# The context's products with group B's input columns in a pass of their own, the S5 units beside the latent tokens' pass

## The chip, the cores and the metric

The kernel runs on one core of one Trainium2 chip. The time is the device time of one execution in microseconds (us), the median of three runs. Every engine (TensorE, VectorE, ScalarE, GpSimd, SyncE) works through its own queue of instructions in order, and waits at an instruction whose inputs aren't there yet.

## The reference

One layer of a network over 1024 latent tokens with 2048 features and 256 context tokens. Cut to what matters:

```
proj_x = modulate(x,   shift_x, scale_x) @ w_in          # 1024 x 2048 @ 2048 x 5120
ub_c   = modulate(ctx, shift_c, scale_c) @ w_in[:, B]    # 256 x 2048 @ 2048 x 1024
u, v, za, ub_x, zb = split(proj_x)                       # 1024 columns each
ya = u' * (w_s @ LN(v') + b) * silu(za)                  # group A: position mixing in 8 heads
yb = S5(ub_x, ub_c)                                      # group B: 64 groups, scan in both directions,
                                                         #   latent scans start from the context's state
yb = glu(yb) * silu(zb)
gate = silu(c) @ w_ada[:, 4096:] + b_ada[4096:]          # one row of 2048
out = LN(alpha * x + gate * (concat(ya, yb) @ w_out)) * ln_g + ln_b
```

So the weights' columns of group B (ub) are multiplied with the latent tokens and with the context; the S5 scan needs both products.

## The kernel before, in words

**Products.** All large products are float32 split in two parts: ScalarE copies a raw chunk of weights to a rounded part (`whi`), VectorE subtracts it from the raw chunk to get the rest (`wlo`). The inputs have such parts too (`xT` for the latent tokens, `cT` for the context, each a pair). A k-step is three passes: hi x hi, hi x lo, lo x hi. A chunk of weights is 128 x 1024 (512 KB) and holds 8 k-steps of one block of 128 output columns; a block is two chunks. `block` (L827) does one block for the two halves of the latent tokens: two PSUM banks of 128 x 512 (tag `mm`), so six matmuls of 512 columns for a k-step. With `extra` it adds a third bank (tag `sb`), and three matmuls of 256 columns for a k-step.

**Weights.** `Weights` (L547 on) loads raw chunks on SP's queue and splits them. `wget` (L654) hands out a chunk, issues the load two chunks ahead and the split of the next chunk. There are two buffers each for `whi`, `wlo` and the raw chunk, so the split of the next chunk waits until the matmuls of the one before the present are done.

**Order of the blocks** in the input projection: four of v, the first of zb, eight of ub (group B), four of v, then u and za of each head in turn, then the rest of zb. Behind them come the GLU and the output projection.

**Side tasks.** Everything beside the weights' matmuls is written as generators. `pump` (L672) moves each task on by one step after each k-step. A model of the engines' clocks (`ck.pe`, `ck.dve`, ...) that each issued instruction advances decides when a task goes on: `until(t)` waits for the model's TensorE to reach t, `room` for VectorE to be at most 2500 ns ahead. `drain` (L691) pumps the tasks without issuing a block in between, and advances the model's TensorE clock by 1300 ns each time. All of this happens when the kernel is built; on the chip the order on each engine is fixed.

The tasks that matter here:
- `bias_task` (L1044): for each of 8 heads a load of w_sp (`ws`, two buffers) and b_sp (`bs`, one buffer), a matmul with ones, one VectorE operation, and a store on ScalarE's queue.
- `gate_task` (L1058): the gate's row. Loads of 512 KB of w_gate, one VectorE multiply-add per 128 rows of it into `acc`, at the end of a stretch of columns a matmul that adds up the partitions.
- `ub_evac` (L1092): after each ub block ScalarE copies the three banks to `us` and stores it in scratch with eight DMAs on its own queue (tile `tmp_ub`).
- `s5_task` (L1111): first the S5 tables (some 300 small VectorE operations, results to scratch), then 32 units of two groups each. A unit on VectorE: `make_w`, `make_e`, `make_t`, `rot`, `scan`, `back`. On TensorE: `pe_b` (input products, 24 matmuls `sb<-uu,uw`), `pe_z` (taps, 30 small matmuls into `sy`), `pe_y` (outputs, `sy<-uu,uk` and `sy<-us,ut`). A unit reads its input `uu` from `tmp_ub`. This task starts behind the last ub block, beside the second half of v.

In the ub pass the code reads

```
    tasks.append(bias_task())
    for m in range(8):
        o, e = block(("ub", m), extra=cxT)
        ub_evac(m, o, e)
        if m == 0:
            tasks.append(gate_task())
    drain()
```

Of the kernel before, what the change touches and what calls it, by code (L numbers as in the profile page):

```python
# [13 lines left out]
OP = mybir.AluOpType  # L14
# [573 lines left out]
def build(tc, a, out, scratch):  # L588
# [32 lines left out]
    col0 = {"u": 0, "v": 8, "za": 16, "ub": 24, "zb": 32}  # L621
# [30 lines left out]
    W.alloc_raw = lambda i: wpool.tile([128, 1024], FT, name="wraw", tag="whi" if i == 2 else "wraw")  # L652
# [174 lines left out]
    def block(key, order=(0, 1), extra=None):  # L827
        o = [bank("mm", 4) for _ in range(2)]
        e = bank("sb", 2) if extra else None
        n = 0  # L830
        for c in order:
            hi, lo = wget((key, c))
            for kk in range(8):
                k = 8 * c + kk
                wt = (hi[:, kk * 128:kk * 128 + 128], lo[:, kk * 128:kk * 128 + 128])
                bs = list(zip(o, xT))
                if extra:
                    bs.append((e[:, :256], extra))
                kstep(bs, wt, k, n == 0, n == 15)
                n += 1  # L840
                pump()
        return o, e
# [191 lines left out]
    o, _ = block(("v", 3))  # L1034
    vb.append(o)
    o, _ = block(("zb", 0))
# [6 lines left out]

# [14 lines left out]
    def gate_task():  # L1058

        for c in range(2):  # L1060
            cols = slice(1024 * c, 1024 * c + 1024)
            acc = st_p.tile([128, 1024], FT, name="acc", tag="sta")
            w = {}

            def load(i):
                w[i] = (st_p.tile([128, 1024], FT, name="gw", tag="stb") if i % 2 else
                        us_p.tile([128, 1024], FT, name="gw", bufs=1))
                SP.dma_start(w[i], a["w_gate"][i * 128:i * 128 + 128, cols])
            load(0)
            for i in range(16):  # L1070
                if i < 15:
                    load(i + 1)
                yield from wait(2)
                if i:
                    V.scalar_tensor_tensor(acc, w[i], sc[:, 0, i:i + 1], acc, op0=OP.mult, op1=OP.add)
                else:
                    V.tensor_scalar(acc, w[0], sc[:, 0, 0:1], None, op0=OP.mult)
                yield
            br = us_p.tile([128, 1024], FT, name="gw", bufs=1)
            SP.dma_start(br[0:1], a["b_gate"][None, cols])  # L1080
            yield from wait(3)
            yield from until(ck.dve + 2000)
            for h in halves:
                ps = bank("ps", 1)
                T.matmul(ps, ones, acc[:, h], start=True, stop=True)
                yield from wait(2)
                V.tensor_add(br[0:1, h], ps[0:1], br[0:1, h])
            SP.dma_start(scratch["gate"][None, cols], br[0:1])
# [3 lines left out]
    def ub_evac(m, o, e):  # L1092
        us = us_p.tile([128, 8, NK], FT, name="us", bufs=1)
        S.activation(us[:, :, 0:KC].rearrange("p j k -> p k j"), e[:, :256].rearrange("p (k j) -> p k j", j=8), AF.Copy)
        for h in range(2):
            S.activation(us[:, :, KC + 64 * h:KC + 64 * h + 64].rearrange("p j k -> p k j"),
                         o[h].rearrange("p (k j) -> p k j", j=8), AF.Copy)
# [10 lines left out]
    cx_es.close()  # L1108


    def s5_task():  # L1111
# [22 lines left out]
        for u in range(3):  # L1134
            s5.load_u(u)
# [39 lines left out]
        def outputs(u):  # L1175
            yield from after(u, tk)
            yield from until(max(tb[u], tk[u]) + 700)
            yield from bank_held()
            s5.pe_y(u)
            yield from until(ck.pe + 500)  # L1180
            s5.evac_y(u)
            if u + 3 < NU:
                s5.load_u(u + 3)
            held.clear()
            out_.add(u)

# [44 lines left out]
    tasks.append(s5t)  # L1231

# [3 lines left out]
    def head_in(h):  # L1236
        vh = s2.tile([128, 8, 128], FT, name="vh")
# [12 lines left out]
    def head_out(h, ug, zs):  # L1250
        vh, ws, bp = hv.pop(h)
        yield from wait(2)
        for c in range(2):
# [4 lines left out]
            tm = s2.tile([128, 4, 128], FT, name="tm")  # L1258
# [16 lines left out]
    for m in range(4, 8):  # L1275
        o, _ = block(("v", m))
        start(v_last(o) if m == 7 else v_out(m, o))
    for h in range(8):
        o, _ = block(("u", h))
# [3 lines left out]
        o, _ = block(("za", h))  # L1283
# [25 lines left out]
    for m in range(1, 8):  # L1309
        if m == 7:  # L1310
            drain(s5t)
            s5_es.close()
            sb_open()
            s2_es.close()
            tasks.append(y5_task(g1_es.enter_context(tc.tile_pool(name="g1", bufs=1))))
        o, _ = block(("zb", m))
        if m == 1:
            drain(ho)
        zb_out(m, o)
# [252 lines left out]
```

## Time and profile before

| | us |
|---|---|
| median of 3 runs | 1667.15 (1666.43 to 1670.48) |
| profiled execution | 1667.93 |
| its span, first to last instruction | 1666.2 |
| TensorE busy | 1602.8 (96%) |
| VectorE busy | 1048.7 (63%) |
| ScalarE busy | 510.1 (31%) |
| GpSimd busy | 157.3 (9%) |

The profile's names: PE is TensorE's matmuls, PEld its weight loads, DVE VectorE, ACT ScalarE, POOL GpSimd; ACTq and SPq are DMA issues on ScalarE's and SyncE's queues. All engine instructions go through one helper and so have the line L521; they are told apart by their tiles, written output<-input. A matmul's duration holds its way through the array, and matmuls overlap: their pace is read from their starts. PEclk is the clock granted to TensorE as a share of 2.4 GHz. In order of time the blocks of group B (with `cT`) lie between 213 and 443 us, the tables between about 454 and 566 us, the S5 units between 566 and 1175 us.

### The profile page before, as it was taken

What the parts mean: (1) busy time and instruction counts of PE and PEld (TensorE: products, weight loads), DVE (VectorE), ACT (ScalarE), POOL (GpSimd) and SP (SyncE); (2) the same over time, 40 slices, a digit from 0 to 9 for tenths busy, and PEclk for the clock granted to TensorE, in tenths of its full rate; (3) what the DMA queues carried; (4) which work ended last, traced back from release to release, by engine and by line L of the source; (5) the groups of instructions that cost most, each with busy time, mean ns of one, the idle gap of its engine ahead of it and who ended that gap; (6) DMA issues with size and microseconds to landing.
All of it is one profiled execution on the core that took longest, in us unless ns stands there. A gap on an engine that the chain in (4) does not pass through costs nothing.

```text
span 1666.2 us, 23176 instructions
## 1 busy us (share of the span) xinstructions
PE 1602.8 (96%) x9056; PEld 1298.0 (78%) x9056; DVE 1048.7 (63%) x1914; ACT 510.1 (31%) x833; POOL 157.3 (9%) x214
## 2 busy tenths in 40 slices
PE   4999999999999899999999999999999999999995
PEld 1556888888878788788888888777888888887895
DVE  8542613332299598988988888896376544456447
ACT  2544631111121322332233323223443412133222
POOL 0000000000000021212212211122000000012004
PEclk9999999999999999999999999999999999999998
DMA  9885325444223533443444344333445533365332
GB/s 336 311 315 201 115 90 173 146 150 157 85 77 131 161 112 102 130 121 98 136 110 117 110 134 119 107 106 104 159 141 171 200 101 127 133 221 180 100 119 101
DMA packets 119494, 241.80 MB, mean 145 GB/s; under 512 B 33364, under 2 KB 63188, under 8 KB 117592
## 3 DMA queue, kind: packets, MB, share of 16 engines
q1 hardware_dynamic: 94808, 215.88, 39.4%
q10 hardware_dynamic: 14336, 14.68, 2.7%
q0 software_dynamic: 10240, 9.76, 2.5%
q8 instruction: 71, 1.16, 0.3%
q14 instruction: 39, 0.32, 0.1%
HBM read 203.97 MB, written 36.12 MB: 144 GB/s over the span
## 4 chain that ended last, share of the span: by engine, by line
PE 79%; DVE 7%; DMA 7%; issue 3%; ACT 2%; SPq 1%; ACTq 1%; POOL 0%; POOLq 0%; DVEq 0%
PE mm L521 56%; PE sb L521 10%; PE sy L521 8%; PE ps L521 4%; DMA uk<-tmp_z 3%; DMA tmp_z<-zs 1%; DMA wraw<-in_w_out_dram 1%; DVE wlo L521 1%; DVE lnw L521 1%; DVE stats L521 1%; DVE z L521 1%; ACT whi L521 1%; DVE t L521 1%; DVE xn L521 1%; DMA xn<-in_x_dram 1%
## 5 line engine op out<-in xcount | busy, mean ns | idle before, releaser
L521 PE MATMUL mm<-xT,whi 128*128 128x512 f32 x2496 | 717.3, 401 | 2.1 <-ACT whi L521 1.2
L521 PEld LDWEIGHTS mm<-xT,whi 128*128 128x128 f32 x2496 | 442.4, 189 | 99.2 <-issue 7.0
L521 DVE TENSOR_TENSOR wlo<-wraw,whi 128x1024 fp32r<-128x1024 f32 (+1 forms) x156 | 191.6, 1230 | 393.6 <-ACT whi L521 390.6
L521 PE MATMUL mm<-xT,wlo 128*128 128x512 f32 x1248 | 393.9, 393 | 3.3 <-DVE wlo L521 3.2
L521 ACT ACTIVATE whi<-wraw 128x1024 fp32r<-128x1024 f32 (+1 forms) x156 | 161.4, 1036 | 428.6 <-PE mm L521 197.2
L521 PEld LDWEIGHTS mm<-xT,wlo 128*128 128x128 f32 x1248 | 227.0, 189 | 52.2 <-DVE wlo L521 4.6
L405 POOL DMA_DIRECT2D tmp_z<-zs x64 | 42.5, 669 | 708.5 <-DVE uw L521 579.2
L521 PE MATMUL mm<-whi,ya 128*128 128x512 f32 (+1 forms) x320 | 83.5, 347 | 0.0
L521 PE MATMUL mm<-whi,yb 128*128 128x512 f32 (+1 forms) x320 | 83.5, 347 | 0.0
L521 POOL TENSOR_TENSOR z<-z,lnb 128x1024 f32<-128x1024 f32 (+1 forms) x16 | 36.8, 2307 | 452.1 <-ACT z L521 452.1
L521 PE MATMUL sb<-cT,whi 128*128 128x256 f32 x256 | 72.9, 285 | 0.0
L521 PE MATMUL mm<-y,whi 128*128 128x512 f32 x256 | 68.4, 389 | 0.0
L521 PEld LDWEIGHTS mm<-whi,yb 128*128 128x128 f32 x320 | 56.4, 189 | 7.5
L521 PEld LDWEIGHTS mm<-whi,ya 128*128 128x128 f32 x320 | 56.4, 189 | 7.4
L477 POOL DMA_DIRECT2D tmp_y<-ys x64 | 38.6, 608 | 233.7 <-ACT ys L521 232.9
L521 PE MATMUL sy<-ada,cs 128*32 128x512 f32 x256 | 41.4, 630 | 19.4 <-DMA ada<-in_w_mod_dram 19.4
L521 ACT ACT_TABLE_LOAD x39 | 50.0, 1283 | 32.6 <-issue 29.8
L521 PEld LDWEIGHTS sb<-uu,uw 128*64 128x64 f32 x768 | 46.7, 140 | 15.5 <-issue 10.5
L521 DVE SCALAR_TENSOR_TENSOR acc<-gw,sc,acc 128x1024 f32<-128x1024 f32 x30 | 38.5, 1283 | 30.8 <-DMA gw<-in_w_gate_dram 30.6
L521 PEld LDWEIGHTS sb<-cT,whi 128*128 128x128 f32 x256 | 47.9, 187 | 10.7
L521 PE MATMUL mm<-wlo,yb 128*128 128x512 f32 (+1 forms) x160 | 55.7, 348 | 0.3 <-DVE wlo L521 0.3
L521 PEld LDWEIGHTS mm<-y,whi 128*128 128x128 f32 x256 | 48.0, 188 | 10.0
(262 smaller groups left out, 2287.2 us busy)
## 6 DMA issues: line engine op xcount, KB each, us to landing
wraw<-in_w_in_dram SPq DMA_DIRECT2D x77, 512.0 KB
ada<-in_w_mod_dram SPq DMA_DIRECT2D x64, 512.0 KB
wraw<-in_w_out_dram SPq DMA_DIRECT2D x56, 512.0 KB
gw<-in_w_gate_dram SPq DMA_DIRECT2D x32, 512.0 KB
xn<-in_x_dram SPq DMA_DIRECT2D x16, 512.0 KB
upf<-tmp_pf SPq DMA_DIRECT2D x32, 256.0 KB
ubb<-in_b_c_dram SPq DMA_DIRECT2D x32, 256.0 KB
tmp_ub<-us ACTq DMA_DIRECT2D x64, 80.0 KB
```

The costliest lines, as they stand in the source:

```text
L405: nc.gpsimd.dma_start(dap(d["z5"], (z["g0"] + q) * 32 * 144, [[72, 2], [144, 32], [1, 72]]), zs[64 * q:64 * q + 64])
L477: nc.gpsimd.dma_start(dap(d["y5"], (g0 + g) * 16384, [[128, 8], [1024, 16], [1, 128]]), ys[:, g])
L521: r = f(*args, **kw)
```

## The change

The order of the blocks gets eight more, `cx`, between zb 0 and ub. They have the same weights as ub. A `cx` block does the context's products alone (three matmuls of 256 columns for a k-step), so group B's weights are loaded and split twice. Each `cx` block is copied to `usc` and stored with eight DMAs of its own, each ub block likewise with eight. A third raw buffer (`craw`) serves every third chunk of the `cx` pass. `bias_task` runs beside the `cx` blocks, `s5_task` and `gate_task` start before the first ub block; a unit's load of `uu` is issued only when the ub block that it reads has been stored (`ub_there`). The gate's row is made in four stretches of 512 columns instead of two of 1024, with half the length of each VectorE operation and twice as many. Behind the last ub block `drain(gt_)` issues steps of all tasks until the gate's task has ended.

```
-    blocks = ([("v", m) for m in range(4)] + [("zb", 0)] + [("ub", m) for m in range(8)]
+    blocks = ([("v", m) for m in range(4)] + [("zb", 0)] + [("cx", m) for m in range(8)] + [("ub", m) for m in range(8)]
...
+    def wraw(i):
+        if i % 3 == 2 and first[("cx", 0), 0] + 3 < i <= first[("cx", 7), 1]:
+            return us_p.tile([128, 1024], FT, name="craw", bufs=1)
+        return wpool.tile([128, 1024], FT, name="wraw", tag="whi" if i == 2 else "wraw")
+    W.alloc_raw = wraw
...
-        for c in range(2):
-            cols = slice(1024 * c, 1024 * c + 1024)
-            acc = st_p.tile([128, 1024], FT, name="acc", tag="sta")
+        for c in range(4):
+            acc = s2.tile([128, 512], FT, name="acc", tag="tm")
...
+                for j in range(2):
+                    k = 2 * i + j
+                    if k:
+                        V.scalar_tensor_tensor(acc, w[i][:, j], sc[:, 0, k:k + 1], acc, op0=OP.mult, op1=OP.add)
...
             yield from until(ck.dve + 2000)
...
+            T.matmul(ps, ones, acc, start=True, stop=True)
...
+    def ub_out(m, us, k0, n):
         for j in range(8):
-            S.dma_start(dap(scratch["ub"], (8 * m * 128 + 16 * (7 - j)) * NK, [[128 * NK, 8], [NK, 16], [1, NK]]), us[:, j])
+            S.dma_start(dap(scratch["ub"], (8 * m * 128 + 16 * (7 - j)) * NK + k0, [[128 * NK, 8], [NK, 16], [1, n]]),
+                        us[:, j])
     tasks.append(bias_task())
     for m in range(8):
-        o, e = block(("ub", m), extra=cxT)
-        ub_evac(m, o, e)
-        if m == 0:
-            tasks.append(gate_task())
+        e = bank("sb", 2)
+        for c in range(2):
+            hi, lo = wget((("cx", m), c))
+            for kk in range(8):
+                wt = (hi[:, kk * 128:kk * 128 + 128], lo[:, kk * 128:kk * 128 + 128])
+                kstep([(e[:, :256], cxT)], wt, 8 * c + kk, c + kk == 0, c == 1 and kk == 7)
+                pump()
+        us = us_p.tile([128, 8, KC], FT, name="usc")
+        S.activation(us.rearrange("p j k -> p k j"), e[:, :256].rearrange("p (k j) -> p k j", j=8), AF.Copy)
+        ub_out(m, us, 0, KC)
     drain()
...
         for u in range(3):
+            yield from ub_there(u)
             s5.load_u(u)
...
     s5t = s5_task()
     tasks.append(s5t)
+    gt_ = gate_task()
+    tasks.append(gt_)
+    for m in range(8):
+        o = block(("ub", m))
+        us = s2.tile([128, 8, KL], FT, name="us", tag="vh")
+        for h in range(2):
+            S.activation(us[:, :, 64 * h:64 * h + 64].rearrange("p j k -> p k j"),
+                         o[h].rearrange("p (k j) -> p k j", j=8), AF.Copy)
+        ub_out(m, us, KC, KL)
+        ub_m.append(m)
+    drain(gt_)
```

What this makes of the order on the engines is shown at three places. First ScalarE's queue around the end of a block of group B, before (`us` is the copy of the banks, `tmp_ub` its store, `whi` the split of the next chunks):

```order
L521 ACTIVATE us<-sb 128x32x8
L521 ACTIVATE us<-mm 128x64x8 x2
L1099 DMA tmp_ub<-us 8x16x160 x8
L521 ACTIVATE whi<-wraw 128x1024
L1056 DMA tmp_bp<-bs 128x128
L521 ACTIVATE whi<-wraw 128x1024
```

and in the `cx` pass of the changed kernel (with the buffers' numbers; `usc` is the copy of the context's bank):

```order
L521 ACTIVATE usc_2169<-sb_2106 128x32x8
L1092 DMA tmp_ub<-usc_2169 8x16x32 x8
L521 ACTIVATE whi_2182<-wraw_2139 128x1024
L521 ACTIVATE whi_2212<-craw_2180 128x1024
L521 ACTIVATE usc_2240<-sb_2179 128x32x8
L1092 DMA tmp_ub<-usc_2240 8x16x32 x8
L521 ACTIVATE whi_2253<-wraw_2210 128x1024
```

Eight issues and two splits stand between two copies as before. TensorE has 48 matmuls of 256 columns for them in the `cx` pass, where a block before had 96 of 512 and 48 of 256.

Second VectorE. Before, in the first S5 unit, the splits of the weights (`wlo`) stand between the unit's parts:

```order
L521 TENSOR_TENSOR wlo<-wraw,whi 128x1024
L521 TENSOR_TENSOR ut<-utab,uc 128x320 x2
L521 TENSOR_TENSOR p_4349<-utab,uc 128x320 x2
L521 TENSOR_TENSOR ut<-ut,p_4349 128x320 x2
L521 TENSOR_TENSOR p_4348<-sb,ue 128x640
L521 TENSOR_TENSOR p_4349<-sb,ue 128x640
L521 TENSOR_TENSOR p_4348<-p_4348,p_4349 128x640
L521 TENSOR_TENSOR uw<-upf,ubb 128x512
```

In the changed kernel, within `drain(gt_)`, parts of the units (`uw` is make_w, `p<-ur` the scan, `us` back, `ue` make_e) and of the gate (`acc`) follow each other:

```order
L521 SCALAR_TENSOR_TENSOR acc<-gw,sc,acc 128x512 x2
L521 TENSOR_TENSOR uw<-upf,ubb 128x512
L521 TENSOR_TENSOR ubb<-upf,ubb 128x2x2x128
L521 TENSOR_TENSOR uw<-uw,ubb 128x256 x2
L521 SCALAR_TENSOR_TENSOR p_3570<-ur,p_3569 128x640
L521 SCALAR_TENSOR_TENSOR acc<-gw,sc,acc 128x512 x2
L521 TENSOR_TENSOR p_3569<-p_3570,ue 128x4x128
L521 TENSOR_TENSOR p_3570<-p_3570,ue 128x4x128
L521 TENSOR_TENSOR us<-p_3569,p_3570 64x512
L521 TENSOR_TENSOR us<-p_3569,p_3570 64x4x128
L521 TENSOR_TENSOR ue<-utab 128x320 x2
```

No split of weights stands among them: between the split of the first chunk behind the ub blocks and that of the second lie 67 rows of this kind.

Third TensorE behind the last ub block. Before, the next block follows at once (`sb<-cT` is the context's last matmul, the rows behind it are the next block's):

```order
L521 MATMUL mm<-xT,whi 128x512 x2
L521 MATMUL sb<-cT,whi 128x256
L521 MATMUL mm<-xT,wlo 128x512 x2
L521 MATMUL sb<-cT,wlo 128x256
L521 MATMUL mm<-xT,whi 128x512 x4
L521 MATMUL mm<-xT,wlo 128x512 x2
```

In the changed kernel the units' and the gate's matmuls stand there (a part of them; `bblk` and `dsk` are taps, `uk` and `us` outputs, `uw` input products, `acc` the gate):

```order
L521 MATMUL sb<-uu,uw 64x32
L521 MATMUL sy<-uu,uk 128x128
L521 MATMUL sy<-us,ut 128x128 x2
L521 MATMUL sy<-uu,uk 128x128
L521 MATMUL sy<-us,ut 128x128 x2
L521 MATMUL sy<-ut,bblk_3561 32x72 x8
L521 MATMUL sy<-ut,bblk_3561 32x16 x4
L521 MATMUL sy<-dsk,eye 32x16 x2
L521 MATMUL ps<-acc,io 128x512
L521 MATMUL sb<-uu,uw 64x160
```

In all, three groups of `sb<-uu,uw`, three of outputs, two of taps and the gate's matmul stand there with no `mm<-xT` among them.

## Rows read from the trace of the kernel before

**Rows 1.** Busy time by stage: PE, PEld, DVE, ACT, POOL, clock, DMA share, GB/s.
```profile
214.00:444.00 230.00, 230.00 (x1175) 194.07 (x1174) 63.77 (x61) 38.01 (x43) 0.00 (x0) 1.00 0.43 139
454.00:566.00 112.00, 107.30 (x485) 88.17 (x483) 89.80 (x321) 28.19 (x45) 0.00 (x0) 0.98 0.35 115
566.00:1175.00 609.00, 596.93 (x4137) 489.85 (x4138) 516.51 (x858) 188.23 (x387) 119.84 (x192) 0.99 0.41 115
```

**Rows 2.** PE in order of time, a ub block: start us, us, operation.
```profile
269.93 0.63 PE L521 MATMUL mm<-xT,whi 128*128 128x512 f32 x2
...
271.69 0.63 PE L521 MATMUL mm<-xT,whi 128*128 128x512 f32 x2
```

**Rows 3.** PE in order of time, a block without context.
```profile
445.73 1.07 PE L521 MATMUL mm<-xT,whi 128*128 128x512 f32 x4
...
447.09 1.07 PE L521 MATMUL mm<-xT,whi 128*128 128x512 f32 x4
```

**Rows 4.** PE in order of time, matmuls of 256 columns late in the output projection.
```profile
1603.87 0.40 PE L521 MATMUL mm<-whi,yb 128*128 128x256 f32 x2
...
1604.23 0.40 PE L521 MATMUL mm<-whi,yb 128*128 128x256 f32 x2
```

**Rows 5.** ACT in order of time around a ub block's end, idle before in brackets.
```profile
257.86 9.61 ACTq L1056 DMA_DIRECT2D tmp_bp<-bs  x2
270.13 0.64 ACT L521 ACTIVATE us<-sb 128x256 f32<-128x256 f32 x1 [13.82 <-PE sb L521]
270.55 2.09 ACT L521 ACTIVATE us<-mm 128x512 f32<-128x512 f32 x2
272.68 5.04 ACTq L1099 DMA_DIRECT2D tmp_ub<-us  x8
277.77 1.06 ACT L521 ACTIVATE whi<-wraw 128x1024 fp32r<-128x1024 f32 x1 [5.12 <-DMA tmp_ub<-us]
```

**Rows 6.** DVE in order of time, the split behind it.
```profile
278.86 1.23 DVE L521 TENSOR_TENSOR wlo<-wraw,whi 128x1024 fp32r<-128x1024 f32 x1 [9.45 <-ACT whi L521]
```

**Rows 7.** Busy time by stage around two stalls of TensorE, columns as in rows 1.
```profile
488.00:492.00 4.00, 0.76 (x4) 0.33 (x3) 3.94 (x5) 1.48 (x3) 0.00 (x0) 1.00 0.01 2
493.00:497.00 4.00, 4.00 (x15) 3.18 (x14) 3.90 (x6) 0.60 (x1) 0.00 (x0) 0.57 0.31 117
563.00:568.00 5.00, 1.54 (x7) 0.94 (x5) 0.59 (x1) 1.21 (x3) 0.00 (x0) 1.00 0.88 229
568.00:575.00 7.00, 5.61 (x31) 5.00 (x32) 6.86 (x16) 2.24 (x4) 0.00 (x0) 0.51 0.65 224
```

**Rows 8.** DVE by shape, 566 to 1175 us: busy us, mean ns, idle before.
```profile
L521 DVE TENSOR_TENSOR wlo<-wraw,whi 128x1024 fp32r<-128x1024 f32 x42 | 51.4, 1224 | 72.3 <-ACT whi L521 69.4 <-DMA utab<-tmp_tab 2.9
L521 DVE TENSOR_TENSOR p<-sb,ue 128x640 f32<-128x640 f32 x64 | 49.9, 817 | 3.7 <-ACT ue L521 3.7
L521 DVE TENSOR_TENSOR ut<-utab,uc 128x320 f32<-128x320 f32 x64 | 28.4, 484 | 0.0
L521 DVE SCALAR_TENSOR_TENSOR tm<-ps,vecs,bp 128x512 f32<-128x512 f32 x16 | 12.0, 748 | 3.9 <-PE ps L521 3.8
L521 DVE TENSOR_TENSOR tm<-tm,ug 128x512 f32<-128x512 f32 x16 | 11.1, 692 | 0.6
```

**Rows 9.** The page's group of the gate's multiply-adds.
```profile
L521 DVE SCALAR_TENSOR_TENSOR acc<-gw,sc,acc 128x1024 f32<-128x1024 f32 x30 | 38.5, 1283 | 30.8 <-DMA gw<-in_w_gate_dram 30.6
```

**Rows 10.** PE in order of time, matmuls of S5 units.
```profile
681.34 1.53 PE L521 MATMUL sb<-uu,uw 128*64 128x160 f32 x24
...
687.02 0.38 PE L521 MATMUL sy<-uu,uk 128*128 128x128 f32 x2
...
687.91 0.61 PE L521 MATMUL sy<-us,ut 128*128 128x128 f32 x4
692.58 0.69 PE L521 MATMUL sy<-ut,bblk 128*32 128x72 f32 x24
```

**Rows 11.** PE's waits: us in total, times, longest.
```profile
PE sy L521 <- DMA uk<-tmp_z: 8.6, 9, 2.5
```

More of the change, by code (lines that the diff above doesn't have):

```diff
@@ L825, in kstep, with block @@
                          skip_group_check=True)
-    def block(key, order=(0, 1), extra=None):
+    def block(key, order=(0, 1)):
         o = [bank("mm", 4) for _ in range(2)]
-        e = bank("sb", 2) if extra else None
         n = 0
@@ L1033, in build @@
     tasks.append(ct)
-    o, _ = block(("v", 3))
+    o = block(("v", 3))
     vb.append(o)
-    o, _ = block(("zb", 0))
+    o = block(("zb", 0))
     drain()
@@ L1069, in gate_task @@
             load(0)
-            for i in range(16):
-                if i < 15:
+            for i in range(8):
+                if i < 7:
                     load(i + 1)
                 yield from wait(2)
[L1074 to L1079, printed above, removed]
@@ L1080, in gate_task @@
-            SP.dma_start(br[0:1], a["b_gate"][None, cols])
-            yield from wait(3)
-            yield from until(ck.dve + 2000)
[L1083 to L1097, printed above, removed]
+                for j in range(2):
+                    k = 2 * i + j
+                    if k:
+                        V.scalar_tensor_tensor(acc, w[i][:, j], sc[:, 0, k:k + 1], acc, op0=OP.mult, op1=OP.add)
+                    else:
+                        V.tensor_scalar(acc, w[i][:, j], sc[:, 0, 0:1], None, op0=OP.mult)
+                    yield
@@ L1098, in ub_evac @@
+            br = st_p.tile([128, 2, 512], FT, name="gw", tag="sta")
+            SP.dma_start(br[0:1, 0], a["b_gate"][None, 512 * c:512 * c + 512])
+            yield from until(ck.dve + 2000)
+            ps = bank("ps", 1)
+            T.matmul(ps, ones, acc, start=True, stop=True)
+            yield from wait(2)
+            V.tensor_add(br[0:1, 0], ps[0:1], br[0:1, 0])
+            SP.dma_start(scratch["gate"][None, 512 * c:512 * c + 512], br[0:1, 0])
+    def ub_out(m, us, k0, n):
         for j in range(8):
-            S.dma_start(dap(scratch["ub"], (8 * m * 128 + 16 * (7 - j)) * NK, [[128 * NK, 8], [NK, 16], [1, NK]]), us[:, j])
+            S.dma_start(dap(scratch["ub"], (8 * m * 128 + 16 * (7 - j)) * NK + k0, [[128 * NK, 8], [NK, 16], [1, n]]),
+                        us[:, j])
@@ L1108, in build, with ub_there @@
     cx_es.close()
+    ub_m = []
+    def ub_there(u):
+        while len(ub_m) <= u * GU // 8:
+            yield
     def s5_task():
@@ L1181, in outputs @@
             s5.evac_y(u)
-            if u + 3 < NU:
-                s5.load_u(u + 3)
             held.clear()
             out_.add(u)
+            if u + 3 < NU:
+                yield from ub_there(u + 3)
+                s5.load_u(u + 3)
         def weights(u):
@@ L1282, in build @@
             S.activation(ug[:, halves[c]], o[c], AF.Gelu)
-        o, _ = block(("za", h))
+        o = block(("za", h))
         zs = st_p.tile([128, 1024], FT, name="zs", tag="stb")
@@ L1315, in build @@
             tasks.append(y5_task(g1_es.enter_context(tc.tile_pool(name="g1", bufs=1))))
-        o, _ = block(("zb", m))
+        o = block(("zb", m))
         if m == 1:
```

23 lines of the change are left out of this document (9 added, 14 removed).

## The prediction

> **What bounds the kernel now.** I read the busy time by stage first, then TensorE's order of time, then what ScalarE and VectorE do at the places that the change touches. The stages [rows 1] show TensorE busy throughout: 230.00 of 230 us in the pass over group B's input columns (214 to 444 us), 596.93 of 609 us in the stage of the S5 units (566 to 1175 us). There is little idle time to win: some 17 us between 454 and 1190 us, besides the two ends of the program. VectorE is the second engine: 516.51 of 609 us beside the units, 89.80 of 112 us beside the tables (454 to 566 us), but only 63.77 of 230 us in group B's pass. So in that pass VectorE and ScalarE have room, and later VectorE has hardly any. The change rearranges that room: the context's products get a pass of their own in front, and tables, units and the gate's row all move beside what is left of the pass.
>
> **Part 1: the context's matmuls leave the blocks.** In order of time [rows 2] one k-step (six matmuls of 512 columns, three of 256) goes from 269.93 to 271.69 us: 1.76 us, 1.755 over several. A plain k-step, from 445.73 to 447.09 us, takes 1.36 us [rows 3]. Over 8 blocks of 16 k-steps the blocks lose 128 x (1.755 - 1.36) = 50.6 us.
>
> **Part 2: the context's own pass.** It has 384 matmuls of 256 columns. Such matmuls alone, each with its own weights, start every 0.12 us (three from 1603.87 to 1604.23 us) [rows 4], so the pass would take 46 us if weights were always ready. They are not. A chunk of weights now lasts 24 x 0.12 = 2.9 us, where it lasted 14 us. At a block's end ScalarE's queue holds, as the rows of the order under the change show, the copy of the bank, eight DMA issues, and only behind them the whi split of the next block's second chunk. Before [rows 5]: the copy starts at 270.13 us (0.64 us), the eight issues hold the queue for 5.04 us, whi starts at 277.77 us and takes 1.06 us; the wlo split follows at 278.86 us for 1.23 us [rows 6]. Without the two copies of the latent banks (2.09 us) that is 0.7 + 5.0 + 0.1 + 1.1 + 1.2 = 8.1 us from the end of one block until wlo of the next block's second chunk is there; the first chunk has covered 2.9 us of it. Behind wlo come 22 matmuls (2.6 us) and the semaphores and drain (0.3 us, an estimate from the gaps in these rows). So a block takes 11.0 us, not 5.8. The first one takes about 9.4, since ScalarE still has the activation of block zb 0 in front of its second chunk: 9.4 + 7 x 11.0 = 86 us.
>
> With gaps of 4 to 5 us in every block the clock comes in. After TensorE had stood still in 488 to 492 us (busy 0.76 us) the granted clock was 0.57 in 493 to 497 us, and after the gap in 563 to 568 us it was 0.51 in 568 to 575 us [rows 7]: mostly the lower level, 1.2 GHz. The matmuls behind wlo then cost up to twice as much, 1.0 to 2.6 us a block; I take 10 us for seven blocks. The Trainium skill (TensorE: Matmul & The Clock Gate, Part 1) says that the low clock is the default and that activity releases it; by that rule the whole pass could stay low, and the rows agree as far as they go.
>
> The eight small rows of the bias (w_sp and b_sp) now fall into the first three blocks. Each needs its own load, a matmul, a VectorE operation and a store, and one bs buffer serves all; before, two of their stores held ScalarE's queue for 9.61 us [rows 5]. Nothing shows them at this pace: 0 us if they fit into the gaps, 20 us if half of such a wait (9.61 us / 2 = 4.8 us for one) comes on top for each of the eight; I take 4. The pass: 86 + 10 + 4 = 100 us, bounds 86 and 125.
>
> **Part 3: the drain behind the last ub block.** The loop over the eight blocks is followed by drain(gt_), which issues tasks with no weights' matmul between until the gate's task has ended. The order shows what falls in there on TensorE: three groups of input products, three of outputs and two of taps of the S5 units, and a matmul of the gate. They wait for VectorE, which has there three each of make_w, scan and back, and two each of rot, make_e and make_t, and 14 gate operations. A unit's VectorE time is (516.51 - 51.4 for 42 splits - 34 for the 16 halves of heads) / 32 = 13.5 us [rows 1, 8]; three units less one rot (three rows of about 0.82) and one make_e and make_t (twelve of 0.484) are 40.5 - 8.3 = 32 us. A gate operation on 512 columns lies between half of 1283 ns and 748 ns [rows 8, 9], 14 x 0.7 = 10 us. A further 2 us are the waits that one unit has on the other engines. So TensorE is held for some 44 us, and 1.3 us for the last output. Of these the matmuls themselves (B 1.5, Y 1.5, Z 0.9 us) [rows 10] make 3 x 1.5 + 3 x 1.5 + 2 x 0.9 = 11 us that are only moved here. Net 34 us; with the recovering clock behind so long a gap (some 3.5 to 7 us at the lower level [rows 7], which cost half of that) 37, and 2 us since ScalarE comes to its parts behind block 7's eight issues: 39 us. Bounds: 25 if VectorE is one unit ahead when TensorE arrives, 55 if it is as late as part 4 allows.
>
> **Part 4: tables and gate beside the ub blocks.** At every block edge whi of the second chunk still stands behind two copies and eight issues: 2.1 + 5.0 + 1.1 = 8.3 us. VectorE takes its work in order, so it stands still at wlo meanwhile, as it did for 9.45 us in [rows 6], where it had nothing else to do. Now it has: tables (89.80 us less some 18 for splits and statistics [rows 1]) 72, three quarters of the gate 34, 16 splits 20, two units 27, in all 153 us, in 174 us of ub matmuls and some 8 of units. Spare are 29 us; seven edges of 8.3 us take 58. The excess of 29 us reaches TensorE where it waits for VectorE: at the gate's matmuls, the units' and the splits. Splits are issued a chunk ahead, which absorbs some: I take 22, bounds 0 and 50.
>
> **Part 5: what is won behind.** The units end eight blocks earlier, and the last ten blocks of the input projection run without them. TensorE's waits for uk, 8.6 us in all [rows 11], may fall elsewhere; I take 3 us off (0 to 12). The 16 more splits cost VectorE 20 and ScalarE 17 us and SP 16 loads; they are in the parts above, and the loads (8 MB in the 100 us of part 2 are no more than 84 GB/s, where the whole core moved 139 GB/s in group B's pass [rows 1]). SP's queue now has the loads of tables and units between the ub weights' loads; these are issued two chunks (22 us) ahead, so I cost that at nothing, and a chunk's 11 us if a wait there outlasts the lead. The wait that is added (a unit's load waits until its block's store is issued) holds nothing up: a block serves four units, and four units take over 50 us of VectorE where a block takes 22 us.
>
> **Sum**, against the profiled execution's own 1667.9 us (span 1666.2): -50.6 + 100 + 39 + 22 - 3 = +107, so 1775 us; the median of the runs is 0.8 us lower, which changes nothing here.
>
> **The rivals.** *The context's pass runs dense,* because an issue of a small store doesn't hold ScalarE's queue as before. A copy of 0.64, whi 1.06, wlo 1.23 us and waits then come to 3.1 us, just covered by a chunk. The Trainium skill (DMA: Bandwidth & Descriptors, Anatomy of one DMA) gives some 50 ns for the sequencer to dispatch a DMA, by which the eight issues would be 0.4 us. Then part 2 is 50 us, part 4 nearly nothing, and the time 1667.9 - 51 + 50 + 39 - 3 = 1703 us. Against it stand the 5.04 us for eight issues of the same pattern of 8 x 16 rows [rows 5]. Chance 0.10.
> *VectorE's lag adds up.* The bias chain holds every block, part 4 is at its upper end, and TensorE's clock stays low through the pass: 125 + 55 + 50 in the places of 100, 39 and 22: 1844 us. Chance 0.08.
> *The earlier start pays, on the other side.* If VectorE runs ahead far enough through the ub blocks to have its part of the drain done when TensorE arrives, parts 3 and 4 vanish; it decides from some 40 us of lead on. With a dense pass the time is 1667.9 - 51 + 48 - 17 (all stalls between 454 and 1190 us) = 1648 us. For it: VectorE's idle share of group B's pass. Against it: each wlo waits for a buffer that TensorE frees, so VectorE is never more than a chunk or so ahead. Chance 0.04; and 0.02 that gains and losses cancel within 0.3% (5 us, about what can be told from no change here).
> *Only the drain is hidden* (the gate's task ends early in real time): the order on each engine is fixed when the kernel is built, so this can't be, and it has no chance of its own.
>
> **How the numbers follow.** My forecast has 0.76: 1775 us, own range from the terms' bounds taken two at a time, 1725 to 1830. The dense pass below it and the lag above it widen the range to 1710 to 1832, which leaves some 0.1 out on either side. Faster 0.04, same 0.02, slower 0.94.
>
> **What would show it.** In the context's pass TensorE busy about half the time, waits for ScalarE's whi and VectorE's wlo once per block, edges 11 to 14 us apart, ScalarE's queue full of issues. Behind the last ub block a hole of some 40 us in which only sb<-uu, sy and ps matmuls run, and the lower clock after it. In the ub blocks VectorE idle at wlo for whi seven times. The units over some eight blocks earlier. Wrong would be: block edges 6 us apart in the context's pass, or no 40 us hole.

## The result and the profile after

| | before | after |
|---|---|---|
| median, us | 1668.82 (4 runs, 1666.43 to 1671.0) | 1781.54 (4 runs, 1780.0 to 1784.12) |
| profiled execution, its span | 1667.93, 1666.2 | 1780.91, 1779.1 |
| TensorE, VectorE busy | 1602.8, 1048.7 | 1637.7, 1072.5 |

The change makes the kernel slower by 6.7%: the ratio is 1.0672, 95% interval 1.0652 to 1.0692. The forecast was 1775 us.

First the busy time by stage after (columns as in [rows 1]): the context's pass, the ub blocks, the hole between the last ub block and v 4, and the units up to their end.

```profile
211.80:327.90 116.10, 72.13 (x401) 67.72 (x400) 22.57 (x27) 24.84 (x31) 0.00 (x0) 0.77 0.33 99
327.90:551.50 223.60, 199.82 (x964) 160.43 (x963) 161.72 (x403) 40.63 (x56) 8.38 (x13) 0.94 0.52 156
551.50:596.40 44.90, 20.59 (x169) 16.07 (x167) 43.64 (x75) 7.83 (x19) 9.41 (x16) 0.60 0.54 148
596.40:1104.40 508.00, 504.35 (x3497) 413.08 (x3496) 439.54 (x759) 154.87 (x334) 100.98 (x162) 1.00 0.42 115
```

In the pass TensorE works 72 of 116 us, at a mean granted clock of 0.77. VectorE, which had room in group B's pass [rows 1], now works 205 of the 268 us between the first ub block and v 4 (161.72 + 43.64). Behind v 4 TensorE is busy 504 of 508 us.

The three bounds of these stages (first context matmul, first ub matmul, first matmul of v 4) and the end of the input projection divide the 113 us. The table has the same four marks for every kernel that was run; each is the start of a matmul in the trace of the profiled execution.

| kernel | median, us | ratio to before (95%) | context's pass | first ub to v 4 | v 4 to end of projection |
|---|---|---|---|---|---|
| before | 1668.8 | | | 230.4 | 763.4 |
| after | 1781.5 | 1.0672 (1.0652 to 1.0692) | 116.2 | 268.4 | 722.3 |
| e1_cx_alone | 1749.8 | 1.0472 (1.0427 to 1.0517) | 116.6 | 194.0 | 762.2 |
| e2_cx_pool | 1741.8 | 1.0428 (1.0404 to 1.0451) | 76.8 | 270.5 | 721.2 |
| e3_bias | 1771.4 | 1.0604 (1.0575 to 1.0632) | 105.4 | 268.8 | 719.5 |
| e4_gate | 1778.1 | 1.0643 (1.0618 to 1.0668) | 117.4 | 243.0 | 739.7 |
| e5_defer | 1769.9 | 1.0606 (1.0590 to 1.0623) | 116.8 | 256.5 | 721.2 |
| e6_gate_store | 1782.1 | 1.0677 (1.0659 to 1.0696) | 116.3 | 271.6 | 720.5 |
| e7_all | 1715.1 | 1.0275 (1.0250 to 1.0300) | 56.3 | 258.8 | 720.6 |
| e8_gate_split | 1713.4 | 1.0255 (1.0226 to 1.0284) | 92.4 | 209.4 | 737.0 |
| e9_gate_late | 1739.0 | 1.0411 (1.0389 to 1.0432) | 117.2 | 215.6 | 728.9 |
| e10_all_late | 1661.6 | 0.9944 (0.9926 to 0.9962) | 55.6 | 206.8 | 726.3 |
| e11_late_units | 1672.2 | 1.0009 (0.9995 to 1.0022) | 57.8 | 177.8 | 764.4 |
| e12_ub_at_once | 1677.3 | 1.0050 (1.0033 to 1.0066) | 55.7 | 218.0 | 726.0 |

From before to after: +116.2 for the pass, +38.0 up to v 4, -41.1 behind it, together 113.1 us.

**The context's pass.** Its blocks take 10.2, 21.3, 19.6, 13.5, 12.3, 12.9, 13.1 and 13.1 us. In order of time, a block end of the steady part (start us, us, engine, operation, idle before):

```profile
276.74 0.62 ACT L521 ACTIVATE usc<-sb 128x256 f32<-128x256 f32 x1 [3.43 <-PE sb L521]
277.39 4.96 ACTq L1092 DMA_DIRECT2D tmp_ub<-usc  x8
279.75 0.28 PE L521 MATMUL sb<-cT,wlo 128*128 128x256 f32 x1
282.40 1.06 ACT L521 ACTIVATE whi<-wraw 128x1024 fp32r<-128x1024 f32 x1 [5.04 <-DMA tmp_ub<-usc]
283.49 1.22 DVE L521 TENSOR_TENSOR wlo<-wraw,whi 128x1024 fp32r<-128x1024 f32 x1 [8.93 <-ACT whi L521]
283.51 0.50 PE L521 MATMUL sb<-cT,whi 128*128 128x256 f32 x2 [3.48 <-ACT whi L521]
284.77 0.58 PE L521 MATMUL sb<-cT,wlo 128*128 128x256 f32 x1 [0.76 <-DVE wlo L521]
```

This answers to [rows 5, 6]: the copy, eight issues of 4.96 us, and only then whi. TensorE uses up the first chunk by 280.03 us and stands until 283.51. Its waits in the whole pass (us in all, times, longest):

```profile
PE sb L521 <- ACT whi L521: 25.0, 6, 5.4
PE sy L521 <- DMA ws<-in_w_sp_dram: 8.5, 3, 4.0
PE sy L521 <- DVE bs L521: 4.9, 2, 4.5
PE sb L521 <- DVE wlo L521: 3.4, 6, 0.8
PE sy L521 <- issue: 2.1, 1, 2.1
```

The second and third rows are the bias. It holds ScalarE and SP as well. On ScalarE in order of time (the first row is two issues of 0.33 us, at 240.83 and 245.75 us, and between them the wait for the second one's row):

```profile
240.83 5.26 ACTq L1056 DMA_DIRECT2D tmp_bp<-bs  x2
246.13 0.62 ACT L521 ACTIVATE usc<-sb 128x256 f32<-128x256 f32 x1 [8.73 <-DVE bs L521]
```

and SP's longest wait of the pass is for the store of the one bs buffer:

```profile
SPq L1050 <- DMA tmp_bp<-bs: 34.3, 7, 6.3
```

**From the first ub block to v 4.** VectorE's waits up to the last ub block:

```profile
DVE wlo L521 <- ACT whi L521: 31.8, 5, 10.8
DVE acc L521 <- DMA gw<-in_w_gate_dram: 22.9, 5, 11.3
DVE bblk L521 <- DMA tmp_pf<-qi: 4.4, 1, 4.4
```

205 us of work and these 59 us of standing are 264 of the 268 us. Such a sum by itself shows nothing: in group B's pass of the kernel before, VectorE worked 64 us and stood 162 of the 230, with TensorE busy throughout. What is new is that VectorE has three times the work, and still stands for ScalarE's issues and for the gate's loads. The longest of these waits for whi at the edge of a ub block, 9.80 us, is behind eight issues that took twice as long as in the steady part of the pass:

```profile
448.99 10.98 ACTq L1092 DMA_DIRECT2D tmp_ub<-us  x8
460.02 1.06 ACT L521 ACTIVATE whi<-wraw 128x1024 fp32r<-128x1024 f32 x1 [11.06 <-DMA tmp_ub<-us]
461.11 1.22 DVE L521 TENSOR_TENSOR wlo<-wraw,whi 128x1024 fp32r<-128x1024 f32 x1 [9.80 <-ACT whi L521]
```

In the hole VectorE has no wait at all, while TensorE waits for it and works at half clock. That VectorE sets the pace of the whole stretch is what e5, e9 and e10 test below. Two stretches of the hole, columns as in [rows 1], and TensorE's first three waits:

```profile
551.50:557.50 6.00, 1.91 (x26) 1.42 (x24) 5.84 (x10) 1.96 (x2) 1.81 (x4) 1.00 0.68 199
557.50:591.60 34.10, 15.70 (x121) 11.90 (x123) 33.25 (x57) 5.88 (x17) 7.60 (x13) 0.50 0.55 145
```

```profile
PE sy L521 <- DVE ut L521: 6.9, 2, 3.8
PE sb L521 <- DVE uw L521: 6.1, 2, 4.5
PE sy L521 <- DVE us L521: 4.3, 2, 2.5
```

**Behind v 4.** 41.1 us less: up to v 4 the kernel has now done six units' input products, five units' outputs and five units' taps, which stood behind v 4 before: 6 x 1.5 + 5 x 1.5 + 5 x 0.9 = 21 us at the prediction's prices from [rows 10]. The other 20 us are stalls that the kernel before had there, and the low clock behind them. The whole stretch from v 4 to the end of the projection, before and after: TensorE without work for 16.8 and 3.7 us, mean clock 0.99 and 1.00.

```profile
443.00:1206.40 763.40, 746.63 (x4810) 613.08 (x4809) 619.62 (x1191) 234.52 (x450) 119.84 (x192) 0.99 0.41 118
596.40:1318.70 722.30, 718.64 (x4457) 591.09 (x4457) 479.75 (x799) 201.70 (x393) 102.19 (x164) 1.00 0.37 107
```

### The profile page after: what moved, and what is told of

It is laid out like the page before. It is cut to its first block, busy times and chain, and to the rows that moved or that the text cites. A ratio compares the mean times of both kernels' runs of the same rounds, so it can differ in the third digit from the quotient of the medians.

```text
span 1779.1 us, 23349 instructions
## 1 busy us (share of the span) xinstructions
PE 1637.7 (92%) x9056; PEld 1326.3 (75%) x9056; DVE 1072.5 (60%) x1962; ACT 511.8 (29%) x837; POOL 157.5 (9%) x214
## 4 chain that ended last, share of the span: by engine, by line
PE 58%; DVE 10%; DMA 9%; issue 4%; ACT 3%; ACTq 2%; POOL 0%; SPq 0%; POOLq 0%; DVEq 0%
PE mm L521 44%; PE sb L521 7%; PE sy L521 5%; DMA uk<-tmp_z 3%; PE ps L521 3%; ACTq L1092 2%; DMA tmp_z<-zs 2%; DVE wlo L521 1%; DVE acc L521 1%; ACT whi L521 1%; DVE p L521 1%; DMA wraw<-in_w_out_dram 1%; DVE t L521 1%; DVE z L521 1%; DMA tmp_ub<-us 1%
## 5 line engine op out<-in xcount | busy, mean ns | idle before, releaser
L521 PE MATMUL mm<-xT,whi 128*128 128x512 f32 x2496 | 701.2, 401 | 2.2 <-ACT whi L521 1.1
L521 PEld LDWEIGHTS mm<-xT,whi 128*128 128x128 f32 x2496 | 461.4, 190 | 108.7 <-issue 7.0
L521 DVE TENSOR_TENSOR wlo<-wraw,whi 128x1024 fp32r<-128x1024 f32 (+1 forms) x168 | 206.3, 1230 | 477.1 <-ACT whi L521 468.8
L521 ACT ACTIVATE whi<-wraw 128x1024 fp32r<-128x1024 f32 (+1 forms) x168 | 173.6, 1037 | 490.3 <-PE mm L521 253.6
L521 PEld LDWEIGHTS mm<-xT,wlo 128*128 128x128 f32 x1248 | 236.0, 189 | 56.2 <-DVE wlo L521 4.6
L521 PE MATMUL sb<-cT,whi 128*128 128x256 f32 x256 | 65.0, 354 | 25.0 <-ACT whi L521 25.0
L521 PEld LDWEIGHTS sb<-cT,whi 128*128 128x128 f32 x256 | 54.6, 260 | 26.3 <-ACT whi L521 26.3
L521 PE MATMUL sb<-uu,uw 128*64 128x160 f32 (+2 forms) x768 | 52.2, 278 | 14.3 <-issue 8.2
L521 PE MATMUL mm<-wlo,yb 128*128 128x512 f32 (+1 forms) x160 | 55.7, 348 | 0.5 <-DVE wlo L521 0.5
L521 PE MATMUL mm<-wlo,ya 128*128 128x512 f32 (+1 forms) x160 | 55.6, 347 | 0.2 <-DVE wlo L521 0.2
```

What stands on the lines that cost most here:

```text
L521: r = f(*args, **kw)
```

## The experiments

Each is an edit of the changed kernel; times and stages are in the table above.

**What the pass costs by itself.** e1 starts the units behind the ub pass, as before; the gate's task has one step less per load.

```
     gt_ = gate_task()
     tasks.append(gt_)
...
     drain(gt_)
+    s5t = s5_task()
+    tasks.append(s5t)
...
-                yield from wait(2)
+                yield from wait(1)
```

> The context's pass alone: the units' task starts behind the ub pass as in the kernel before, and the gate's task takes one step less per load, so that it is done within the ub blocks and the drain is empty. Theory (the pass costs what the changed kernel's trace shows, 116 us, and the blocks lose 51): TensorE reaches v 4 at about 212 + 116 + 8 x 22 = 504 us where the kernel before reached it at 443, and the rest is as before: about 1668 + 61 = 1729 us, between 1722 and 1740. Rival (most of the 113 us come from the tables and units moving forward): 1668 to 1690 us.

1749.8 us: more than both had it. The pass (116.6) and the stretch behind v 4 (762.2) are as the theory said, but the ub pass takes 194 us, not 176. Even without the units TensorE waits there for the gate:

```profile
PE ps L521 <- DVE acc L521: 10.7, 3, 4.8
```

Much of the rest is low clock (mean 0.96). Most of the loss is the pass; early units add 28 us to it (1778.1 - 1749.8, against e4 below, which has the same gate).

**What holds the pass.** e2 issues the context's stores on GpSimd's queue; e3 gives the bias rows more buffers.

```
-        ub_out(m, us, 0, KC)
+        ub_out(m, us, 0, KC, P)          # e2: issued by GpSimd, not by ScalarE
...
-            ws = us_p.tile([128, 128], FT, name="ws")
+            ws = us_p.tile([128, 128], FT, name="ws", bufs=3)          # e3
-            bs = us_p.tile([128, 128], FT, name="bs", bufs=1)
+            bs = us_p.tile([128, 128], FT, name="bs", bufs=4)          # e3
```

> The changed kernel with the 64 stores of the context's products issued on GpSimd's queue, which is idle there, instead of ScalarE's. Theory (the eight issues between the copy and the next whi split hold every block of the pass): block edges from 12.3 to 13.5 us apart down to 6 to 8, the pass from 116 to 60 to 75 us, the time from 1781 to 1730 to 1742 us. Rival A (the lower clock and the weight loads set the pace of the pass, the issues lie beside them): pass over 105 us, time 1770 to 1783. Rival B (the loads of 512 KB per chunk bound it as soon as the issues are gone): edges 9 to 11 us, pass 85 to 95, time 1750 to 1760.

> The changed kernel with four buffers for bs and three for ws, where there were one and two. Theory (the slow blocks 1 and 2 of the pass, 21.3 and 19.6 us, wait for the bias rows, one behind the other through one buffer): these blocks come to 12 to 14 us, the time from 1781 to 1766 to 1771 us. Rival (they are slow because ScalarE's queue holds the bias stores and TensorE runs at half clock there, which buffers don't change): 1778 to 1783 us.

e2: pass 76.8 us, 39.4 less, and the time 39.8 less: the theory's mechanism, with the pass 1.8 us longer than its range. The last five blocks take 6.6, 6.3, 5.8, 5.7 and 5.8 us. At a block end the eight issues now stand beside the matmuls:

```profile
272.25 0.64 ACT L521 ACTIVATE usc<-sb 128x256 f32<-128x256 f32 x1 [1.94 <-DMA tmp_ub<-usc]
272.67 1.07 ACT L521 ACTIVATE whi<-wraw 128x1024 fp32r<-128x1024 f32 x1
273.18 4.69 POOL L1092 DMA_DIRECT2D tmp_ub<-usc  x8 [1.63 <-ACT usc L521]
273.77 1.22 DVE L521 TENSOR_TENSOR wlo<-wraw,whi 128x1024 fp32r<-128x1024 f32 x1 [2.21 <-ACT whi L521]
```

Both rivals fall with the stage row of e2's dense part: full clock (1.00) and 183 GB/s, TensorE busy 22.72 of 23 us.

```profile
266.00:289.00 23.00, 22.72 (x190) 22.57 (x189) 10.17 (x9) 10.15 (x12) 18.38 (x32) 1.00 0.69 183
```

The low clock of the pass was thus a consequence of the gaps, not the cause. The Trainium skill (DMA: Bandwidth & Descriptors, Rules for kernel authors) says that spreading DMAs over several engines' queues gives no bandwidth and only saves issue time; here the issue time alone was worth 40 us, because of what stood behind it.

e3: 10.1 us less; blocks 1 and 2 take 15.9 and 14.9 us instead of 21.3 and 19.6. That is the theory's place, at two thirds of its size: ScalarE still issues the bias stores. With those on GpSimd's queue too (e7) the pass takes 56.3 us, 20.5 less than in e2.

**What holds the ub blocks and the hole.** e4 takes one step less between a load of w_gate and its use, so that the gate ends in the last ub block and the drain behind it issues only a group of 12 input products. e5 issues the stores of a ub block one per k-step, behind the whi split. e6 issues the gate's four row stores on GpSimd's queue.

```
-                yield from wait(2)
+                yield from wait(1)               # e4
...
-        ub_out(m, us, KC, KL)
-        ub_m.append(m)
+        tasks.insert(0, ub_later(m, us))         # e5: per step one of the eight, then ub_m.append(m)
...
-            SP.dma_start(scratch["gate"][None, 512 * c:512 * c + 512], br[0:1, 0])
+            P.dma_start(scratch["gate"][None, 512 * c:512 * c + 512], br[0:1, 0])     # e6
```

> The changed kernel with one step less between a load of the gate's weights and its use, so that the gate's task ends in the last ub block and the drain behind the blocks issues only one group of 12 input products. Theory (the hole of 45 us is VectorE's unit work with no weights' matmuls beside it; spread over the v blocks it is hidden there): hole under 5 us, time from 1781 to 1741 to 1752 us. Rival (VectorE's work is only moved and is late in the v blocks instead): the hole goes, but v 4 to v 7 and the u blocks get as much longer, 1768 to 1783 us.

> The changed kernel with the eight stores of a ub block issued one per k-step in the first chunk of the next block, behind the whi split, instead of all at once between the copies and that split. In the changed kernel's ub pass VectorE stands 31.8 us at wlo for whi. Theory (VectorE is the bound beside the ub blocks, so every us that it stands still comes back at TensorE, in the blocks or in the hole behind them): VectorE's wait for whi under 5 us, the time from 1781 to 1749 to 1760 us. Rival (that idle time was spare; VectorE then waits for the gate's loads or the units instead): 1774 to 1783 us.

> The changed kernel with the gate's four stores of one row issued on GpSimd's queue instead of SP's. In the changed kernel SP's queue stands 37.9 us in all (longest 17.8) at these stores, for VectorE's last addition of a stretch, with the next loads of w_gate behind it, and VectorE then stands 22.9 us for these loads. Theory (the queue's order is what makes the loads late): VectorE's wait for gw falls under 10 us, the time from 1781 to 1758 to 1768 us. Rival (the loads are late because of the transfers' own rate, 156 GB/s in this pass): no change, 1776 to 1783 us.

e4 is the rival's case: the hole is gone (1.8 us), and the time is only 3.5 us less, with intervals that overlap. The ub blocks take 18 us longer (572.0 - 330.8 = 241.2, against 223.5), and the stretch behind v 4 17 us, of which 13 are unit products that no longer stand before v 4 (8 us of them instead of 21). TensorE's waits in e4's ub pass:

```profile
PE mm L521 <- DVE wlo L521: 14.4, 6, 7.7
PE sb L521 <- issue: 10.7, 2, 6.8
PE ps L521 <- DVE acc L521: 7.7, 3, 3.8
PE mm L521 <- ACT whi L521: 5.4, 1, 5.4
```

VectorE works 41 us less up to v 4 than in the changed kernel (164.6 against 205.4), but stands 15 us longer. Its lateness, which stood in one hole, is spread over the blocks. So the drain is where the cost showed, not what made it.

e5 lies between the two: 11.6 us less. VectorE's wait for whi fell by 18.5 us, the wait for the gate's loads grew by 6.6:

```profile
DVE acc L521 <- DMA gw<-in_w_gate_dram: 29.5, 7, 9.8
DVE wlo L521 <- ACT whi L521: 13.3, 2, 10.8
```

The difference of 11.9 us is also what the stretch up to v 4 got shorter (256.5 against 268.4). e6 changes nothing (the rival's answer, 1782.1): VectorE still stands 26.0 us at the gate's loads, so SP's stores weren't what made these late. The loads' own time with two buffers may be it; e6 doesn't show that. In e9 below, with four buffers and beside zb, VectorE stands 4.6 us for them, but buffers and place were changed together.

```profile
DVE acc L521 <- DMA gw<-in_w_gate_dram: 26.0, 5, 11.2
```

**All of it, and the gate elsewhere.** e7 is e2, e3, e5 and e6 with the bias stores on GpSimd's queue. e8 also runs two of the gate's four stretches beside the context's pass.

```
-    def gate_task():
+    def gate_task(cs_, pool, n):                 # e8
...
     tasks.append(bias_task())
+    tasks.append(gate_task((0, 1), us_p, 4))     # e8
...
-    gt_ = gate_task()
+    gt_ = gate_task((2, 3), s2, 2)               # e8
```

> The changed kernel with the context's stores, the bias stores and the gate's stores on GpSimd's queue, four bs and three ws buffers, and the ub stores one per k-step behind the whi split. Theory (pass 116 to about 55, bias part included, VectorE's 31.8 and 22.9 us of standing gone, half of it seen at TensorE): 1781 - 60 - 27 = 1694 us, 1670 to 1705. Rival (VectorE's work itself, 205 us in the 268 us from the first ub block to v 4 beside TensorE's 185 us of work, keeps the hole as it is): 1710 to 1725 us.

> As e7_all, and two of the gate's four stretches run beside the context's pass (where VectorE has only the splits), so that the drain behind the ub blocks is empty. Theory (VectorE's work beside the ub blocks is the bound; 17 us of it and the drain leave): hole gone, v 4 reached at about 212 + 62 + 185 = 459 us and the rest 20 us shorter than before: 1655 to 1680 us. Rival (17 MB of weights and gate in a pass of 60 us are more than the transfers give, so the pass gets long): pass 80 to 100 us, 1685 to 1710 us.

e7 is the rival's case, 1715 us: the pass is dense, the hole stays at 46.7 us. VectorE's wait for whi falls to 6.6 us, but that for the gate's loads rises to 33.8. e8 takes the hole away and gets no faster: the pass grows to 92 us, as its rival said, and the time is a little above the rival's range. TensorE there waits 8.6 us for whi, 7.9 for ws and 6.7 for acc, at a mean clock of 0.84:

```profile
213.60:305.00 91.40, 61.47 (x402) 58.13 (x401) 46.16 (x60) 24.47 (x31) 38.51 (x65) 0.84 0.67 212
```

So the gate costs in the pass as well, though VectorE works only 46 of 91 us there; whether by its loads, as the rival has it, isn't settled. e9 puts it where VectorE has room: behind the last unit, beside zb 1 to zb 6, with four buffers and its stores on GpSimd's queue, and takes the drain out. e10 is e7 with that gate.

```
-    gt_ = gate_task()
-    tasks.append(gt_)
...
-    drain(gt_)
...
+        if m == 1:                               # in the loop over zb 1 to zb 7
+            drain(s5t)
+            s5_es.close()
+            gl_es = ExitStack()
+            gt_ = gate_task(gl_es.enter_context(tc.tile_pool(name="gl", bufs=1)))
+            tasks.append(gt_)
         if m == 7:
-            drain(s5t)
-            s5_es.close()
+            drain(gt_)
+            gl_es.close()
```

> The changed kernel with the gate's task out of the ub pass: it starts behind the last unit, beside zb 1 to zb 6, with four buffers for the loads, and no drain stands behind the ub blocks. The context's pass stays as in the changed kernel. Theory (it is VectorE's gate work, 38 us, and its standing for the gate's loads, 23 us, that the ub pass and the hole pay for): no hole, ub blocks of 22 to 24 us, v 4 reached at 513 to 528 us instead of 596, the stretch from there to the end of the input projection some 11 to 20 us longer than 722, time 1725 to 1740 us. Rival (the stalls only move, into the v blocks or to zb 1 to zb 6): 1760 to 1783 us.

> e7_all with the gate's task beside zb 1 to zb 6 as in e9_gate_late. Theory (the pass dense at 56 us against 51 won in the blocks, no stalls beside the ub blocks, and the stalls of 17 us between 454 and 1190 us of the kernel before gone since the units end before the last blocks): 1650 to 1668 us. Rival (the units beside the ub blocks cost what they win): 1672 to 1700 us.

e9: 42.6 us less than the changed kernel, within the theory's range, but not by its steps. v 4 is reached at 545.6 us and not at 513 to 528: the last four ub blocks, where the units are, take 31 to 33 us each instead of 22 to 24, and the stretch behind v 4 is 7 us longer than in the changed kernel, not 11 to 20. Up to v 4 it takes 215.6 us instead of 268.4, and zb 1 to zb 6 lose nothing: TensorE is busy 157 of 157 us there, VectorE 77.5. Its rows from the first ub block to v 4, and beside the gate:

```profile
330.00:545.60 215.60, 200.90 (x1111) 163.66 (x1109) 159.07 (x405) 46.30 (x72) 16.73 (x27) 0.98 0.40 113
1117.00:1274.00 157.00, 157.00 (x694) 128.72 (x693) 77.53 (x97) 31.59 (x38) 2.00 (x4) 1.00 0.56 193
```

VectorE's longest wait beside its ub blocks is still the one for whi:

```profile
DVE wlo L521 <- ACT whi L521: 33.8, 5, 10.5
```

e10: 1661.6 us, the theory's case, faster than the changed kernel by 120 us and than the kernel before by 0.6% (0.9944, interval 0.9926 to 0.9962). The pass, the ub blocks and the units in e10:

```profile
211.50:267.00 55.50, 49.20 (x400) 47.98 (x399) 22.74 (x27) 24.12 (x31) 37.32 (x64) 1.00 0.66 194
267.00:474.00 207.00, 198.75 (x1112) 163.09 (x1110) 159.08 (x405) 45.76 (x72) 21.65 (x36) 0.98 0.43 121
474.00:985.00 511.00, 506.40 (x3519) 415.55 (x3518) 440.67 (x762) 156.63 (x338) 102.07 (x164) 1.00 0.42 115
```

**What the early units are worth, and the block edges once more.** e11 has the units behind the ub pass and the gate as in e1, and e7's other edits except e6's. e12 is e10 with the eight stores of a ub block at once again.

```
-        tasks.insert(0, ub_later(m, us))         # e12, against e10
+        ub_out(m, us, KC, KL)
+        ub_m.append(m)
```

> The dense pass of e7_all, the gate beside the ub blocks (one step less per load), and the tables and units started only behind the ub blocks, as in the kernel before. Theory (the pass costs 56, the blocks lose 51, the gate's matmuls wait 11 us, nothing else changes): 1675 to 1690 us, slower than e10_all_late by some 20 us, which is what the early start of the units is worth. Rival (the early start is worth nothing): within 6 us of e10_all_late.

> e10_all_late with the eight stores of a ub block at once between the copies and the next whi split, as in the changed kernel. Theory (VectorE's standing at wlo costs only where VectorE is the bound; with the gate gone from here it has time to spare before the units begin, and is the bound again only in the last four ub blocks): 1 to 6 us slower than e10_all_late, 1662 to 1668 us. Rival (each block edge costs TensorE by itself, as e5_defer's 12 us over eight blocks could be read): 10 to 15 us slower, 1671 to 1677 us.

e11: 1672.2 us, 10.6 more than e10, between the two expectations. Without early units its ub pass runs at plain pace, TensorE busy throughout, gate included:

```profile
269.00:447.00 178.00, 178.00 (x781) 145.91 (x779) 68.14 (x84) 30.32 (x32) 5.29 (x9) 1.00 0.54 169
```

So a dense pass of its own is about even with the products in the blocks (1.0009 of before), and the early units are worth some 10 us once VectorE isn't overloaded. (e11 and e10 differ also in where the gate stands; in e11's ub pass it can cost 3.7 us at most, 177.8 against eight plain blocks of 174.1.) e12: slower than e10 by 15.7 us (medians) or 18 (the two ratios to before), as the rival had it in size. The place is the theory's: the first four ub blocks take 21.8, 21.8, 23.5 and 21.8 us as in e10 (21.8, 21.8, 23.1, 21.8), and the loss stands in the last four, where the units are. VectorE's wait for whi is 32.5 us (first row) against 17.3 in e10 (second row):

```profile
DVE wlo L521 <- ACT whi L521: 32.5, 7, 10.6
DVE wlo L521 <- ACT whi L521: 17.3, 8, 3.6
```

In the profiled executions v 4 is reached 12.0 us later, and the whole takes 11.0 us longer (1673.5 against 1662.5 us); the rest of the difference of the medians lies in executions without a profile and isn't settled.

## Why the prediction was right, and where its sum was not

The forecast of 1775 us is 6.5 us low, with the right mechanisms in the right places. But terms that were off cancel: against the forecast's +100, -51, +61 (parts 3 and 4) and -3 stand +116, -53, +70 (counted from e11's ub pass) and -20. The places and signs were worked out; that the total came so near is in part luck.

**Part 1** (-50.6): right. In e11, whose ub blocks run without stalls, the ub pass is 52.6 us shorter (230.4 - 177.8).

**Part 2** (100): the pass took 116.2. The steady blocks are as worked out: 11.0 us and the clock for 1.4 made 12.4, the trace has 12.3 to 13.5. The pass didn't stay at the low clock throughout, which the prediction held possible: the mean was 0.77. The mis-sized term is the bias, "I take 4": blocks 1 and 2, where it falls, took 40.9 us, 16 more than two steady ones as forecast, and its removal from ScalarE's queue and from the single buffer was worth 20.5 us, the upper bound given. That bound came from a row read wrongly: the 9.61 us in [rows 5] are two issues of 0.33 us, at 257.86 and 267.14 us, with the wait for the second one's input between them, while ScalarE waited for TensorE anyway. What costs in the pass is such a wait, since a copy stands behind it, as at 246.13 us above; that the bound nearly fits is luck. *The context's pass runs dense* was false for this kernel since the issues do hold the queue (4.96 us against 5.04 in [rows 5]), and came true in the last five blocks of e2, where they stand on another. The Trainium skill (DMA: Bandwidth & Descriptors, Anatomy of one DMA) gives some 50 ns for the dispatch of a DMA, and that for GpSimd's path; an estimate from it, 0.4 us for eight, was carried over to ScalarE's queue in the prediction. The trace has 4.96 us on ScalarE's queue and 4.69 on GpSimd's, and the measurement decides.

**Parts 3 and 4** (39 + 22 = 61): from the first ub block to v 4 the trace has 268.4 us; eight plain blocks (8 x 21.76 = 174.1) and the moved unit products (21) leave 73 (70 by e11's 177.8). The hole's length, 44.9 us, was forecast as 44 + 1.3. The step that failed is its price: "the drain" was charged with 39 us, but without any hole (e4) 61 us are still lost (243.0 - 174.1 - 8 for the fewer products moved). What the runs showed in its place is one cost, VectorE's time between the first ub block and v 4: without the gate there 22 us are left (e9: 215.6 - 174.1 - 19.5), and with 11.6 us of wait for whi up to v 4 instead of 33.8 there are 13 (e10: 206.8 - 174.1 - 19.5). How the gate's 51 us divide into VectorE's work for it and the standing for its loads isn't separated. The prediction counted this excess as 29 us in part 4: it had 58 us of standing for whi in seven waits and none at the gate's loads. The trace has 31.8 us in five waits for whi, 22.9 for the gate's loads and 4.4 for another, together 59, so the total is right by luck.

**Part 5** (-3): -20 us, the other large miss. The prediction had the 17 us of stalls between 454 and 1190 us in its rival of the earlier start, and not in its sum. In e9 and e10, too, the stretch behind v 4 and the moved products together are 748 and 746 us, against 763 before.

**The rivals.** *VectorE's lag adds up* (1844) came true in part: the bias cost nearly what it said, but held two blocks and not every one, and the clock was low for part of the pass only. *The earlier start pays* was wrong for this kernel; its parts, a dense pass and stalls that vanish, are what e10 does at 1661.6 us, though there VectorE has the time because the gate is elsewhere.

## What to carry to other kernels

A hand-over that was cheap at long blocks is a bound at short ones: work out, for the shortest chunk, what stands on each in-order queue between the end of one and the split of the next, and put issues on a queue that nobody waits for. A hole in one engine is priced by the engine that it waits for: count that engine's work over the whole stretch, and the standing that the first engine doesn't cause, before taking the hole away, since otherwise the wait only moves. Work without a deadline (here the gate's row) belongs beside a stage where the second engine is idle and a chunk of weights lasts long (zb, in e9), not where it is first possible and not beside short chunks, where it cost though VectorE was half idle (e8).

## What the runs showed of the hardware that was not expected

An issue of 8 x 16 rows costs its queue about 0.6 us on ScalarE (4.96 us for eight) and as much on GpSimd (4.69), where a plain store of 128 rows took 0.33 us on ScalarE (in the changed kernel, at 225.41 us). The bytes don't make it: eight stores of 16 KB (the context's) and eight of 64 KB (the latent tokens') both take 4.96 us at best. But it isn't fixed either: at the eight edges of the ub blocks of the changed kernel the eight issues took 4.96, 6.29, 7.48, 9.64, 10.98, 6.59, 4.96 and 4.96 us; what made them longer, no run here shows. And the loads of weights kept up with a chunk of 512 KB every 2.9 us, at 183 GB/s, with TensorE busy 22.72 of 23 us.
